# A two-block network with two expert layers on one core: row order and piece size of the expert weights, a two-part combine, a written order of TensorE's work, and a reordered first stage

## The chip, the core and the metric

The kernel runs on one core of one Trainium2 chip. The metric is device time of one execution in microseconds (us). Everything is fp32 data of one sequence: 512 tokens of width 1024, that is 581 MB of DMA traffic in all, most of it weights that are read once.

## What is computed

The network is two blocks in a row. Cut to what matters here:

```python
def first_block(x, ...):                       # one layer
    mod = silu(c) @ w_mod + b_mod              # sh1, s1, g1, sh2, s2, g2
    h = rms_norm(x, norm1_g) * (1 + s1) + sh1
    u = h @ w_pw1 + b_pw1; a, gate = split(u)  # conformer convolution
    u = dwconv(a * sigmoid(gate), w_dw) + b_dw # 31 taps, inside rows of 64 tokens
    y = silu(layer_norm(u)) @ w_pw2 + b_pw2
    x = x + g1 * y
    return x + g2 * (relu(modulated(x) @ w1) ** 2 @ w2)

def second_block(x, ...):                      # two layers
    x = x + g_m * mixer(l, modulated(x))       # l = 0: attention, l = 1: short convolution
    x = x + g_f * ec_moe(modulated(x), router_w, w_gate, w_up, w_down)

def ec_moe(h, w_router, w_gate, w_up, w_down): # 16 experts, each takes its 64 best tokens
    aff = softmax(h @ w_router)
    g, idx = top_k(aff.T, 64)
    xs = h[idx]
    a = silu(xs @ w_gate) * (xs @ w_up)        # 1024 x 1024 for each expert
    y = (a @ w_down) * g
    return zeros(n, d).at[idx].add(y)
```

The three weights of the 16 experts are 201 MB a layer, and all of them are read in every execution.

## The kernel before

**Frame.** The program is written in tiles; a planner places each engine's instructions in an order of its own, by estimated costs and by when the inputs are due. `keep_in_program_order(ins)` pins an instruction behind the one traced before it on the same engine; the kernel before doesn't use it for the experts. PSUM tiles come from two pools, `mm` (6 buffers) and `sm` (2). Large weights go through pages of 8 KB a partition (`wload` L207 to L216: 1 MiB a load, rows 128k to 128k+127, issued by SyncE).

**First stage** (`block1`, L502). Four loads bring x; TensorE transposes it (L515), DVE copies it (L516), ScalarE squares each transposed piece (L517), and eight matmuls with ones sum the squares over the features (L519). L522 to L528 make of that the row factor `rep`. The modulation `mod_now` (L256 matmuls, L263 turned to columns) gives s1 and sh1 by halves, `split` (L389, L390) the two parts of the modulated rows. A product of two fp32 matrices is done in three fp32r matmuls (L435 to L437), after a cast and a subtraction that split the weights (L428, L429). SyncE's loads go in program order: x, w_mod columns 2, 0, two pieces of w_pw1, w_mod 3, the rest of the constants, iota, and later w_mod 1, second pieces of w_pw1 with the bias rows b_pw1 and b_dw between them. b_pw1 is read with one row of 8 KB for each of 128 partitions.

**Convolution** (`conv`, `conv_half`). After the first products the weights of the depthwise convolution (31 x 1024) are loaded by ScalarE's queue into a page, and two matmuls with `taps` (L630) bring them to the frequency domain. `conv_half` (L683) multiplies each tile of 128 tokens (two rows of 64) with a DFT matrix for each row, with all 128 partitions contracted; the matrix holds zeros for the other row.

**Experts** (`moe`, L1292). The 16 experts go in 8 pairs (j, j+8): the two of a pair take the two column halves of TensorE, 64 tokens each. `gather` and `gather_part` select the tokens: a matmul spreads the list of indices (L1350), DVE compares it with iota (L1353, tile `o`), 32 matmuls (64 records) pick the rows (L1364) and DVE applies gain and shift (L1368). `gate_up` makes the gate product, silu (L1416), the up product and act = up * silu(gate) (L1420). `down` transposes act (L1432, ScalarE copies it, L1433), makes the down product, weighs its rows (L1439, L1440) and `combine`s them: 8 matmuls (16 records) add them to the tokens (L1447, L1449). Every product is 8 steps of 4 matmuls 128x64x512 (L1404), and each step waits for its own load from `eload` (L1394): 1 MiB, rows 128k to 128k+127 of both experts, 4 KB a row, one row of each expert to a partition. The pages, three blocks of halves, and two places in the pool of split weights hold these loads; a buffer comes free when its step is done, and SyncE issues the next load into it. The last pair of a layer (`down_last`, matmuls L1471) takes w_d by column halves, so that its first half can be combined while the second is loaded; these loads have pieces of 2 KB (L1391, 512 KB each). In layer 1 the product of the first half is followed by the final additions and the output.

## Time and profile before

| | |
|---|---|
| median of 3 runs | 2200.9 us (2199.98 to 2202.45) |
| the profiled execution | 2200.99 us, its span 2198.9 us |
| mean granted TensorE clock | 0.988 |
| expert stages | about 980 to 1470 us (layer 0), 1690 to 2199 us (layer 1) |
| DMA traffic | 581 MB |

The profile's page is of one execution, with times from the start of its span. A row of the timeline is one instruction or a run of like ones, with what ended the idle time before it in brackets. A window row gives the busy time of TensorE, its weight loads, VectorE, ScalarE and GpSimd (with their instruction counts), then the granted clock of TensorE (1.00 is 2.4 GHz, 0.50 is 1.2 GHz), the mean busy share of the 16 DMA engines, and what they moved in GB/s. An fp32 matmul shows as two records, an fp32r matmul as one. PE is TensorE, DVE VectorE, ACT ScalarE, POOL GpSimd, SP SyncE.

### The profile page before, as it was taken

The page shows a single profiled execution, that of the slowest core. Times are in us where ns is not written, and L with a number is a line of the kernel's source. Part 1 is how long each engine was busy: PE and PEld are TensorE (multiplying, and loading weights), DVE is VectorE, ACT ScalarE, POOL GpSimd, SP SyncE. Part 2 cuts the span into 40 slices and gives each one's busy share as a digit, 9 for nine tenths or more (in the row PEclk, how much of TensorE's full clock was granted, in tenths as well). Part 3 has the DMA queues.
Part 4 walks back from the last instruction along what each step waited for, and adds up shares of the span by engine and source line. Part 5 has one row for each costly group of instructions (what it writes and reads, how often), then busy time and mean ns, then how long its engine had stood idle before and what let it go on. Part 6 is the DMA issues. An engine that isn't in the chain of part 4 may idle for free.

```text
span 2198.9 us, 26994 instructions
## 1 busy us (share of the span) xinstructions
PE 2116.7 (96%) x11010; PEld 1353.5 (62%) x11010; DVE 1004.2 (46%) x1982; ACT 550.6 (25%) x1021; POOL 12.4 (1%) x12
## 2 busy tenths in 40 slices
PE   7999999999999989989999999989998999999998
PEld 4757878788888878765444444338886544444434
DVE  3868996778484579561122122135356122212211
ACT  2334534243343369520000000033232000000001
POOL 0000000000000000000000000010000000000000
PEclk9999999999999999999999999999998999999999
DMA  9715476677311352549999999992263999999996
GB/s 367 253 41 192 170 271 211 207 268 276 130 46 39 84 147 90 173 170 360 394 409 374 398 409 409 409 339 77 96 248 108 348 396 409 375 396 409 409 409 259
DMA packets 204379, 581.23 MB, mean 264 GB/s; under 512 B 12225, under 2 KB 21313, under 8 KB 204000
## 3 DMA queue, kind: packets, MB, share of 16 engines
q1 hardware_dynamic: 203936, 579.00, 70.5%
q8 instruction: 86, 1.41, 0.3%
q10 hardware_dynamic: 320, 0.52, 0.1%
q14 instruction: 37, 0.30, 0.0%
HBM read 571.48 MB, written 2.10 MB: 261 GB/s over the span
## 4 chain that ended last, share of the span: by engine, by line
PE 89%; DVE 4%; DMA 2%; ACT 1%; issue 0%; SPq 0%; DVEq 0%; ACTq 0%
PE mm L1404 29%; PE mm L436 13%; PE mm L435 13%; PE mm L437 13%; PE sm L1364 6%; PE mm L1447 5%; PE mm L1471 1%; PE sm L344 1%; PE tp L1126 1%; DMA b<-w_u 1%; PE sm L689 1%; PE sm L290 1%; DVE mx L1092 1%; PE sm L683 1%; PE sm L1432 1%; PE s L1089 1%
## 5 line engine op out<-in xcount | busy, mean ns | idle before, releaser
L435 PE MATMUL mm<-b,wh 128*128 128x512 f32 (+1 forms) x1136 | 391.6, 346 | 0.6 <-ACT ao L1131 0.5
L436 PE MATMUL mm<-b,wh 128*128 128x512 f32 (+1 forms) x1136 | 391.9, 345 | 0.0
L437 PE MATMUL mm<-b,wl 128*128 128x512 f32 (+1 forms) x1136 | 388.6, 343 | 0.5 <-DVE wl L429 0.5
L429 DVE TENSOR_TENSOR wl<-w,wh 128x1024 fp32r<-128x1024 f32 x160 | 194.1, 1223 | 173.1 <-ACT wh L428 171.9
L1404 PE MATMUL mm<-w,xs 128*64 128x512 f32 x1152 | 259.5, 599 | 0.0
L428 ACT CAST wh<-w 128x1024 fp32r<-128x1024 f32 x164 | 170.1, 1048 | 348.5 <-PE mm L436 266.1
L435 PEld LDWEIGHTS mm<-b,wh 128*128 128x128 f32 x1136 | 216.0, 190 | 39.1 <-issue 9.5
L436 PEld LDWEIGHTS mm<-b,wh 128*128 128x128 f32 x1136 | 216.4, 190 | 34.6 <-issue 9.5
L437 PEld LDWEIGHTS mm<-b,wl 128*128 128x128 f32 x1136 | 215.7, 190 | 28.1 <-issue 3.3
L1404 PE MATMUL mm<-b,xs 128*64 128x512 f32 x864 | 191.8, 593 | 0.0
L242 DVE SCALAR_TENSOR_TENSOR w<-w,sc 128x512 f32<-128x512 f32 x252 | 184.4, 750 | 3.5
L1404 PEld LDWEIGHTS mm<-w,xs 128*64 128x64 f32 x1152 | 82.2, 138 | 156.1 <-issue 148.5
L1420 DVE TENSOR_TENSOR ea<-mm,ea 128x512 f32<-128x512 f32 x32 | 22.1, 692 | 335.7 <-PE mm L1404 284.4
L1364 PEld LDWEIGHTS sm<-o,b 128*128 128x128 f32 x1024 | 121.5, 193 | 63.1 <-issue 55.3
L1364 PE MATMUL sm<-o,b 128*128 128x128 f32 x1024 | 135.6, 285 | 11.9 <-DVE o L1353 11.9
L1404 PEld LDWEIGHTS mm<-b,xs 128*64 128x64 f32 x864 | 67.4, 137 | 117.0 <-issue 102.5
L1368 DVE TENSOR_SCALAR xs<-sm,g_f,m_shf 128x128 f32<-128x128 f32 x128 | 45.9, 405 | 178.5 <-PE sm L1364 178.5
L435 PE MATMUL mm<-wh,b 128*128 128x512 f32 (+1 forms) x320 | 117.0, 370 | 2.9 <-ACT wh L428 2.9
L436 PE MATMUL mm<-wl,b 128*128 128x512 f32 (+1 forms) x320 | 117.8, 368 | 0.1
L437 PE MATMUL mm<-wh,b 128*128 128x512 f32 (+1 forms) x320 | 117.3, 366 | 0.0
L1404 PE MATMUL mm<-w,eaT 128*64 128x512 f32 x512 | 116.8, 598 | 0.0
L1447 PE MATMUL mm<-oT,ey 128*128 128x512 f32 (+1 forms) x248 | 108.1, 586 | 1.6 <-ACT ey L1477 1.6
(339 smaller groups left out, 2296.4 us busy)
## 6 DMA issues: line engine op xcount, KB each, us to landing
w<-w_g SPq DMA_DIRECT2D x80, 1024.0 KB, 17.3
w<-w_d SPq DMA_DIRECT2D x64, 1024.0 KB, 11.9
w<-w_u SPq DMA_DIRECT2D x64, 1024.0 KB, 14.2
b<-w_u SPq DMA_DIRECT2D x60, 1024.0 KB, 9.9
w<-ada_w SPq DMA_DIRECT2D x48, 1024.0 KB, 5.5
b<-w_g SPq DMA_DIRECT2D x48, 1024.0 KB, 16.0
b<-w_d SPq DMA_DIRECT2D x48, 1024.0 KB, 12.3
w<-w SPq DMA_DIRECT2D x32, 1024.0 KB, 6.3
```

Of the source, the lines that this page charges most:

```text
L242: nc.vector.scalar_tensor_tensor(acc, w[:, i], sc, acc, op0=ALU.mult, op1=ALU.add)
L290: nc.tensor.matmul(ps[32 * q:32 * q + 32], self.cst("ones")[:, :32], acc[:, q], start=True, stop=True, skip_group_check=True)
L428: self.nc.scalar.copy(vh, w[:, i:i + kp])
L429: (lo or self.nc.vector).tensor_tensor(vl, w[:, i:i + kp], vh.bitcast(F32), op=ALU.subtract)
L435: mm(out, sh, mh, start=start, stop=False)
L436: mm(out, sh, ml, start=False, stop=False)
L437: mm(out, sl, mh, start=False, stop=stop)
L1364: nc.tensor.matmul(ps[:, 128 * i:128 * i + 128], self.xn[:, t, 128 * k:128 * k + 128], o[:, t], start=(t == 0), stop=(t == 3), skip_group_ ...
L1368: nc.vector.tensor_scalar(xs[:, k], ps[:, 128 * i:128 * i + 128], self.fg[:, k:k + 1], self.fsh[:, k:k + 1], op0=ALU.mult, op1=ALU.add)
L1404: self.nc.tensor.matmul(ps[n][64 * b:64 * b + 64], lhs[:, k, 64 * b:64 * b + 64], w[b][:, 512 * n:512 * n + 512], start=(k == 0), stop=(k ...
L1420: nc.vector.tensor_tensor(act[:, c], up[n], act[:, c], op=ALU.mult)
L1447: nc.tensor.matmul(ps[:, :n], y[:, 128 * f:128 * f + 128], oT[:, t0:t0 + n], start=True, stop=True)
```

## The change

- **Experts, layout.** A partition now holds rows 8p to 8p+7 of a weight. A load brings two of these rows of one expert, 8 KB in one piece for a partition, 32 KB from one partition's piece to the next, and stays 1 MiB; a product waits for the loads of both experts at every second step. The other side of the contraction follows: act and the token-major rows xn are written in permuted columns (strided reads of PSUM in silu, in L1420 and in `token_major`), and gain and shift (`fgs`) are brought into that order through DRAM with three DMAs on GpSimd's queue when the routing begins. The last w_d is loaded in the same row order, pieces of 2 KB as before.
- **Combine.** The weighted rows are split in two fp32r parts (`weigh`: ScalarE writes the high part, VectorE what is left), and each tile takes two fp32r matmuls instead of one fp32 matmul.
- **TensorE's order.** From the end of a layer's first up product to the last pair's transposes, TensorE's expert matmuls are pinned as written: index matmul and first gather block (steps 0 to 3) after the up product, transposes (now in the `mm` pool), down product, second gather block (4 to 7), combine. The index list is padded to 128 partitions with a memset on GpSimd.
- **First stage.** ScalarE squares the token-major x with a running sum, so the sum matmuls L519 and L524 and their copy L522 are gone, and the row factor is made after the fourth transposed piece. The order of the loads changes: w_mod 2, the rest of the constants, w_dw (on ScalarE's queue, into another pool), w_mod 0, first pieces of w_pw1, w_mod 3; later both second pieces of w_pw1 before b_pw1, b_dw and iota. The tap matmuls move into the first stage.
- **DFT.** Each matmul of L683 contracts only the 64 partitions of its own row, in the `mm` pool.

The diff, cut to its core:

```diff
+    def pe(self, ins):
+        if self.pinned:
+            self.tc.keep_in_program_order(ins)
...
+        ms4 = self.sml.tile([128, 4], F32, name="ms4", bufs=1)
+        for t in range(4):
+            nc.scalar.activation(xn[:, 2 * t:2 * t + 2].rearrange("p f t -> p (f t)"), xt[:, t], AF.Square,
+                                 accum_out=ms4[:, t:t + 1])
+        nc.vector.tensor_scalar(ms4, ms4, 1.0 / D, None, op0=ALU.mult)
+        r = self.rsqrt(ms4, 4)
...
+            if f == 3:
+                rep = self.tmp.tile([128, T], F32, name="rep", tag="sl", bufs=2)
+                nc.vector.tensor_copy(rep, self.spread(r, 4))
...
-        ms, mh = [wm(2)], [wm(0)]
+        ms = [wm(2)]
+        nc.sync.dma_start(self.cs[:, NC0:], a["k_cst"][:, NC0:])
+        wd = self.wsp.tile([128, D], F32, name="wd", tag="wl")[:31]
+        nc.scalar.dma_start(wd, a["w_dw"])
+        mh = [wm(0)]
...
         ms.append(wm(3))
-        nc.sync.dma_start(self.cs[:, NC0:], a["k_cst"][:, NC0:])
...
+                rows = self.block(2)
+                for h in range(2):
+                    ps = self.sm_ps()
+                    nc.tensor.matmul(ps[:119], self.cst("taps", 31), wd[:, 512 * h:512 * h + 512], start=True, stop=True)
+                    nc.scalar.copy(rows[:119, 3 * D + 512 * h:3 * D + 512 * h + 512], ps[:119])
                 second = [self.wload(pw[0], 1, 4)]
+                row = lambda v, o, n: nc.sync.dma_start(rows[:, o:o + n], bass.AP(tensor=a[v].tensor, offset=0,
+                                                                                ap=[[0, 128], [1, n]]))
                 second.append(self.wload(pw[1], 1, 4))
+                row("b_pw1", 0, 2 * D)
+                row("b_dw", 2 * D, D)
+                nc.sync.dma_start(self.iota, a["k_iota"])
...
-        wd = self.page()[:31, :D]
-        nc.scalar.dma_start(wd, self.a["w_dw"])
-        for h in range(2):
-            ps = self.sm_ps()
-            nc.tensor.matmul(ps[:119], self.cst("taps", 31), wd[:, 512 * h:512 * h + 512], start=True, stop=True)
-            nc.scalar.copy(gf[:, 512 * h:512 * h + 512], ps[:119])
...
-                    p = self.sm_ps()
-                    o = fo + 119 * b
-                    nc.tensor.matmul(p[:119], self.cs[:, o:o + 119], u[:, t, c], start=True, stop=True)
+                    p = self.mm_ps()
+                    o, q = fo + 119 * b, slice(64 * b, 64 * b + 64)
+                    nc.tensor.matmul(p[:119], self.cs[q, o:o + 119], u[q, t, c], start=True, stop=True)
...
+        rows = self.dram.tile([2, D], F32, name="rows", tag="rows%d" % l)
+        self.fgs = self.sml.tile([128, 2, KT], F32, name="fgs", tag="fgs", bufs=1)
+        for i, v in enumerate((self.fg, self.fsh)):
+            nc.gpsimd.dma_start(rows[i].rearrange("(k p) -> p k", p=128), v)
+        nc.gpsimd.dma_start(self.fgs, rows.rearrange("i (p k) -> p i k", p=128))
...
+            self.best = self.sml.tile([128, 2, CAP], F32, name="best", tag="best", bufs=1)
+            nc.gpsimd.memset(self.best, 0.0)
+            nc.vector.tensor_copy(self.best[:NE], ps[:NE, 128:256].rearrange("p (i s) -> p i s", i=2))
...
+            self.pinned = True
             if j < 7:
                 gs = self.gather(j + 1)
-                for h in range(2):
-                    self.gather_part(gs, 4 * h, 4)
+                self.gather_part(gs, 0, 4)
...
-            self.down(l, j, act, end, after)
+            self.down(l, j, act, end, after, lambda: self.gather_part(gs, 4, 4))
...
-                nc.scalar.activation(self.xn[:, t, 512 * h:512 * h + 512], ps, AF.Copy, scale=r[:, i:i + 1])
+                nc.scalar.activation(self.xn[:, t].rearrange("p (k q) -> p k q", k=KT)[:, :, 64 * h:64 * h + 64],
+                                     ps.rearrange("p (q k) -> p k q", k=KT), AF.Copy, scale=r[:, i:i + 1])
...
-                nc.tensor.matmul(ps[:, 128 * i:128 * i + 128], self.xn[:, t, 128 * k:128 * k + 128], o[:, t],
-                                 start=(t == 0), stop=(t == 3), skip_group_check=True)
+                self.pe(nc.tensor.matmul(ps[:, 128 * i:128 * i + 128], self.xn[:, t, 128 * k:128 * k + 128], o[:, t],
+                                         start=(t == 0), stop=(t == 3), skip_group_check=True))
...
+    def eload(self, src):
+        t = self.eplace()
+        if isinstance(t, list):
+            for k in range(2):
+                self.nc.sync.dma_start(t[k], src[:, k])
+            return t
+        v = t.rearrange("p (k n) -> p k n", k=2)
+        self.nc.sync.dma_start(v, src)
+        return [v[:, k] for k in range(2)]
+
+    def rows(self, name, l, e):
+        return self.a[name][l, e].rearrange("(p k) n -> p k n", k=KT)
...
-            w = self.eload(self.a[name][l, j::8, 128 * k:128 * k + 128, :])
+            if k % 2 == 0:
+                w = [self.eload(self.rows(name, l, j + 8 * b)[:, k:k + 2]) for b in range(2)]
             for n in range(2):
                 for b in range(2):
-                    self.nc.tensor.matmul(ps[n][64 * b:64 * b + 64], lhs[:, k, 64 * b:64 * b + 64],
-                                          w[b][:, 512 * n:512 * n + 512],
-                                          start=(k == 0), stop=(k == KT - 1), skip_group_check=True)
+                    self.pe(self.nc.tensor.matmul(ps[n][64 * b:64 * b + 64], lhs[:, k, 64 * b:64 * b + 64],
+                                                  w[b][k % 2][:, 512 * n:512 * n + 512],
+                                                  start=(k == 0), stop=(k == KT - 1), skip_group_check=True))
...
+        av = act.rearrange("p (k q) -> p k q", k=KT)
         for n in range(2):
-            nc.scalar.activation(act[:, 512 * n:512 * n + 512], gp[n], AF.Silu)
+            nc.scalar.activation(av[:, :, 64 * n:64 * n + 64], gp[n].rearrange("p (q k) -> p k q", k=KT), AF.Silu)
...
-            nc.vector.tensor_tensor(act[:, c], up[n], act[:, c], op=ALU.mult)
+            c = slice(64 * n, 64 * n + 64)
+            nc.vector.tensor_tensor(av[:, :, c], up[n].rearrange("p (q k) -> p k q", k=KT), av[:, :, c], op=ALU.mult)
...
-            ps = self.sm_ps()
+            ps = self.mm_ps()
...
-                nc.tensor.transpose(ps[:, 128 * i:128 * i + 128], act[:, 128 * k:128 * k + 128], self.cst("ident"))
+                self.pe(nc.tensor.transpose(ps[:, 128 * i:128 * i + 128], act[:, 128 * k:128 * k + 128], self.cst("ident")))
...
-        y = self.wsp.tile([128, D], F32, name="ey", tag="wh")
+        y = tuple(self.wsp.tile([128, D], F32R, name="y" + i, tag="w" + i) for i in "hl")
...
         if j == 7:
+            self.pinned = False
         dp = self.product("w_d", l, j, aT)
-        nc.scalar.activation(y[:, :512], dp[0], AF.Copy, scale=w)
-        nc.vector.tensor_scalar(y[:, 512:], dp[1], w, None, op0=ALU.mult)
+        mid()
+        for n in range(2):
+            self.weigh(y, dp[n], w, slice(512 * n, 512 * n + 512))
         self.combine(y, oT, 0, T, range(KT))
+
+    def weigh(self, y, ps, w, c):
+        yh, yl = y
+        self.nc.scalar.activation(yh[:, c], ps, AF.Copy, scale=w)
+        self.nc.vector.scalar_tensor_tensor(yl[:, c], ps, w, yh[:, c].bitcast(F32), op0=ALU.mult, op1=ALU.subtract)
...
-            nc.tensor.matmul(ps[:, :n], y[:, 128 * f:128 * f + 128], oT[:, t0:t0 + n], start=True, stop=True)
+            for i in range(2):
+                self.pe(nc.tensor.matmul(ps[:, :n], y[i][:, 128 * f:128 * f + 128], oT[:, t0:t0 + n],
+                                         start=(i == 0), stop=(i == 1)))
...
+            for i in range(4):
+                v = self.eplace().rearrange("p (e k n) -> p e k n", e=2, k=2)
+                for e in range(2):
+                    nc.sync.dma_start(v[:, e], self.rows("w_d", l, j + 8 * e)[:, 2 * i:2 * i + 2, 512 * n:512 * n + 512])
+                ws.append([v[:, e] for e in range(2)])
```

## Rows read from the trace of the kernel before

**Rows 1.** Page, busy time of each engine over the span (share) and instruction counts.

```profile
PE 2116.7 (96%) x11010; PEld 1353.5 (62%) x11010; DVE 1004.2 (46%) x1982; ACT 550.6 (25%) x1021; POOL 12.4 (1%) x12
```

**Rows 2.** Waits of SyncE over the whole run: engine, line, releaser: total us, times, longest us.

```profile
SPq L1394 <- PE mm L1404: 653.3, 243, 23.4
```

**Rows 3.** Timeline of ScalarE, layer 0 experts: start us, us, instruction, idle before and releaser.

```profile
1001.19 0.60 ACT L1416 ACTIVATE ea<-mm 128x512 f32<-128x512 f32 x1 [29.32 <-PE mm L1404]
...
1060.10 0.60 ACT L1416 ACTIVATE ea<-mm 128x512 f32<-128x512 f32 x1 [20.26 <-PE mm L1404]
...
1312.04 0.60 ACT L1416 ACTIVATE ea<-mm 128x512 f32<-128x512 f32 x1 [20.26 <-PE mm L1404]
...
1372.99 0.60 ACT L1416 ACTIVATE ea<-mm 128x512 f32<-128x512 f32 x1 [20.26 <-PE mm L1404]
...
1423.07 0.60 ACT L1416 ACTIVATE ea<-mm 128x512 f32<-128x512 f32 x1 [20.26 <-PE mm L1404]
```

**Rows 4.** Windows of 10 us, layer 0 experts: busy us per engine, PEclk, DMA share, GB/s.

```profile
1050.00:1060.00 10.00, 10.00 (x50) 3.40 (x48) 0.00 (x0) 0.00 (x0) 0.00 (x0) 1.00 0.89 322
1170.00:1180.00 10.00, 10.00 (x34) 3.85 (x34) 6.86 (x11) 0.00 (x0) 0.00 (x0) 1.00 0.69 247
1240.00:1250.00 10.00, 10.00 (x48) 3.30 (x46) 0.00 (x0) 0.00 (x0) 0.00 (x0) 1.00 0.95 343
1300.00:1310.00 10.00, 10.00 (x48) 3.30 (x46) 0.79 (x3) 0.00 (x0) 0.00 (x0) 1.00 1.03 410
1440.00:1450.00 10.00, 8.89 (x33) 2.73 (x30) 0.00 (x0) 2.75 (x4) 0.00 (x0) 1.00 1.05 386
```

**Rows 5.** Chain of waits at the end of layer 0: start us, us, what.

```profile
1416.94 18.44 DMA b<-w_u
1435.39 10.79 DMA w<-w_d
```

**Rows 6.** Timeline of one pair whose gather stands in one piece, layer 0.

```profile
1076.11 7.41 PE L1364 MATMUL sm<-o,b 128*128 128x128 f32 x64 [0.88 <-DVE o L1353]
...
1084.63 0.65 PE L1432 MATMUL sm<-cs,ea 128*128 128x128 f32 x4 [0.68 <-ACT eaT L1433]
```

**Rows 7.** Chain of waits, layer 0, one combine.

```profile
1169.45 7.06 PE mm L1447 x16
```

**Rows 8.** Chain of waits, convolution stage: matmuls of the split products.

```profile
126.14 0.43 PE mm L437
...
130.97 0.23 PE mm L437
```

**Rows 9.** Windows of 1 to 5 us: start, convolution, end of layer 1.

```profile
24.00:28.00 4.00, 3.65 (x24) 1.37 (x22) 2.50 (x8) 0.24 (x1) 0.00 (x0) 1.00 1.05 386
41.00:42.00 1.00, 1.00 (x8) 0.73 (x5) 0.00 (x0) 0.00 (x0) 0.00 (x0) 1.00 1.05 428
42.00:43.00 1.00, 1.00 (x6) 0.83 (x5) 0.00 (x0) 0.00 (x0) 0.00 (x0) 1.00 1.02 422
120.00:121.00 1.00, 0.00 (x0) 0.00 (x0) 1.00 (x3) 0.00 (x0) 0.00 (x0) 1.00 0.06 25
125.00:130.00 5.00, 5.00 (x12) 3.70 (x12) 0.00 (x0) 0.58 (x1) 0.00 (x0) 0.50 0.79 276
2174.00:2176.00 2.00, 2.00 (x9) 0.60 (x7) 0.27 (x1) 0.00 (x0) 0.00 (x0) 1.00 0.46 171
```

**Rows 10.** Chain of waits, layer 1, first half of the last w_d product.

```profile
2165.01 7.04 PE mm L1471 x32
```

**Rows 11.** Groups by line: matmuls of the DFT and of the taps.

```profile
L683 PE MATMUL sm<-b,cs 128*119 128x512 f32 x32 | 16.1, 610 | 0.0
...
L630 PE MATMUL sm<-w,cs 31*119 31x512 f32 x4 | 2.7, 814 | 3.9 <-DMA w<-w_dw 3.9
```

**Rows 12.** Timeline of the first stage: row factor, first split product.

```profile
26.29 0.69 DVE L528 COPY rep<-sm 128x512 f32<-128x512 f32 x1 [1.25 <-PE sm L378]
...
32.41 2.07 PE L435 MATMUL mm<-wh,b 128*128 128x512 f32 x4 [2.56 <-ACT wh L428]
```

## What was predicted, and how

> **What bounds the kernel now.** I read the page's busy times first: TensorE is busy for 96% of the span, no other engine for half of it [rows 1]. That is an average, so I went to the stages that the change touches most, the two expert stages, and asked who waits for whom. SyncE, which issues the weight loads, waits 243 times for an expert matmul to free a buffer [rows 2]: TensorE is behind, the loads ahead. The first silu of a pair marks its gate product: seven steps from 1001.19 to 1423.07 are 421.9 us, 60.3 each; a pair with its gather in one piece takes 58.9, one whose gather the planner mixed into a product 60.95, the pair without a gather 50.1 [rows 3]. Layer 1 repeats these steps. The windows then show how thin the lead is: three have the DMA below its rate (322, 247, 343), the others stand at 409 to 410 GB/s with a share above 1.0 [rows 4]. A pair needs 24 loads of 1 MiB, 25.17 MB; over 60.3 us that is 417 GB/s, more than the 409 that arrive. So the stage starts on full buffers, is paced by TensorE, and uses up its lead: the chain at the end of layer 0 has 18.4 and 10.8 us of DMA [rows 5]. **Whatever shortens TensorE's pair makes the loads the bound; their rate decides the size of the gain.**
>
> **Experts, TensorE's side.** A gather is 64 records in 7.4 us [rows 6], the combine 16 records in 7.06 us [rows 7]. The two-part combine still has 16 records (two for each of 8 tiles), but of the kind that the split products issue, 0.23 us at the full clock [rows 8]: 3.7 us, 3.4 less a pair. The pin gives back the 2 us by which a mixed pair is longer than one in block order. The transposes in the larger pool lose the 0.7 us wait for the copy of the first four [rows 6]. A pair is then 58.9 - 3.4 - 0.7, about 55 us of TensorE, or 25.17 MB / 55 = 458 GB/s of demand. Two waits are added. The low part of the weighted rows (DVE) waits for the high part (ACT), and behind it on DVE stand the combine's adds, which free TensorE's tiles: some 1.5 us, covered by the gather's second block (half of 7.4), uncovered it would be 1.5 a pair. And the product waits for two loads every second step, so buffers come free later: up to 1 MiB of lead, 2.6 us, once. Strided PSUM reads go to ACT and DVE, which have room [rows 1]. The round trip of the gain rows on GpSimd's queue is issued when the routing begins, long ahead of the first gather, and only a memset stands behind it: nothing; uncovered, a few us a layer.
>
> **Experts, the loads.** The same bytes in the same number of issues, in pieces of 8 KB in place of 4. The nearest rows: pieces of 2 KB run at 386 GB/s, of 4 KB at 409, and the one load with 8 KB pieces (a row that is broadcast) at 428 and 422 [rows 4, 9]. Over 16 engines a piece takes 16 x 2048 / 386 = 85 ns and 16 x 4096 / 409 = 160 ns; another 4 KB on the same slope, 150 ns, makes 310 ns, or 422 GB/s. I take 421, with ends 409 (no gain) and 428. **So the stage becomes DMA-bound:** 421 supplied against 458 wanted. What that gives:
> Idle time of the queue is gone: (409 - 322) / 409 x 10 = 2.1, then 4.0 and 1.6 us from the three windows [rows 4], 7.7 in sum. (A dip in the first pair stays, since the buffers are still full there.)
> Otherwise the queue runs from the first pair, about 1030, to 1435.4 [rows 5]: 397 us x (1 - 409 / 421) = 11.3 us.
> The last w_d keeps its 2 KB pieces. The last combine saves some 3 us in two halves and gives about 1 back to the second weighing step, which nothing covers there: 2.
> Layer 0: -21 us.
> Layer 1: the loads end 7.7 + 11.3 = 19 us earlier. Here TensorE runs behind them to the end: w_d is in by about 2175 [rows 9], so its first half (4.19 MB, 10.8 us at 387) by 2164.2, but the product of that half runs from 2165.0 to 2172.05 without a pause [rows 10]. After the change the half is in by 2145.2 and its product ends one load's matmuls later, 0.9 us, 2146.1; the tail behind it stays: -26 us. TensorE's own limit, 7 x (60.3 - 55) = 37 us less, is not reached in either layer.
>
> **Weights of the depthwise convolution.** TensorE waits 3.9 us for them, and the tap matmuls then take 2.7 [rows 11]. After that pause its granted clock is 0.50, the lower of its two levels [rows 9], and eleven records take 0.43 instead of 0.23 [rows 8], 2.2 us, with half a microsecond more for the one before them. Loaded at the start, all of that goes: -9. The price there: the load moves 25 GB/s at a share of 0.06, one engine of sixteen [rows 9], for about 5 us, in a stretch where all sixteen are full (1.05 [rows 9]); what SyncE queues behind it on that engine can land up to 5 us later. The tap matmuls stand where TensorE waits 2.6 us for ACT [rows 12]; uncovered they cost 1.4 to 2.7 us.
>
> **Row halves in the DFT.** 32 records, 16.1 us [rows 11]. If two 64-row halves run side by side, half of their time, 7 to 8 us, can go; if not, nothing. No row shows such a pair, but the experts' two column halves do run together: 32 records in 7.04 us [rows 10], where the combine needs 7.06 for 16 [rows 7]. DVE, which reads each tile, is next; I take -3.
>
> **First stage.** The sum matmuls and their copy are gone, and the row factor can be there some 3 us before 26.3 [rows 12]. But the large part of the constants now goes in front of w_mod(0) (0.37 MB, 1 us), as does w_dw (up to 5 us); the second loads of w_pw1 pass the bias rows and iota, which are wanted later. Between -3 and +6 I take -1.
>
> **Sum**, against the profiled execution's own 2200.99 us (2.1 us of it outside the span; the median of the runs is 2200.9, so nothing is corrected): 21 + 26 + 9 + 3 + 1 = 60, so 2141 us.
>
> **Rivals.**
> A, larger pieces bring nothing: 409 as before. For it: the queue's share is above 1.0 already. Against: the broadcast row. Then layer 0 keeps 7.7 + 2 = 9.7; in layer 1 the half of w_d is in by 2156.5, its product done by 2157.4, 14.7 less. With 13 from the front: 2201 - 37.4 = 2164.
> The Trainium skill ("DMA: Bandwidth & Descriptors", "Where 436 GB/s comes from") says that between HBM and SBUF the memory side, about 358 GB/s, is what binds. By that no size of piece could help, and the time would be A's; but this trace moves 409 and 428 GB/s [rows 4, 9], above that limit, and the measurement decides.
> B, the loads run at 428: the second term is 397 x (1 - 409 / 428) = 17.6, 6.3 more a layer: 2128, and TensorE's limit lets it go little further.
> C, slower than before. A partition's pieces now lie 32 KB apart, where the old load read 4 KB rows one behind the other. If that pitch costs the queue, each layer pays. At 387 the second term is 397 x (409 / 387 - 1) = +22.6: layer 0 +12.9, layer 1 +7.9, less 13, 2209. The sign turns at about 391 GB/s; at 370 (+42 a layer) it is 2247, and I price C there. Against it: w_mod, whose rows lie 24 KB apart, loads at the same 386 as the last w_d with rows 4 KB apart [rows 4, 9].
> The same page ("Latency and other measured facts") gives 207 GB/s for copies with a row pitch of 512 KiB and less at larger powers of two. No run here shows such a pitch, and 32 KB is not among its cases.
> D, the front gives nothing: the load on one engine holds up the first products, the halves do not pair: 2201 - 47 = 2154.
>
> **Chances.** The forecast (2130 to 2150) 0.60, A 0.15, B 0.10, D 0.08, C 0.07. The range goes to A and B with the unknowns of the front (3 down, 6 and more up) around them: 2118 to 2175. About 0.2%, 4.4 us, is what a measurement can tell here from no change; all cases but C are faster by more, and near C's turning point lies the little that is left: faster 0.91, same 0.02, slower 0.07.
>
> **What would show it.** Right: windows of the expert stages at about 421 GB/s with no dips after the first pair; SyncE's waits for expert matmuls mostly gone, and TensorE's for w_g, w_u, w_d in their place; marks some 59.8 us apart (25.17 / 421); the combine 16 records in 3.7 us; no wait for w_dw and no clock of 0.50 near 125. Wrong: windows at 409 (A), marks nearer 55 (B), windows under 391 (C), the first split product later than 32.4 (D). Wrong altogether: a clock that falls in many short waits for loads, which the DMA-bound end of layer 0 does not show (1.00 at 8.9 us busy of 10 [rows 4]), or a pinned matmul that waits for DVE's adds where the planner had other work.

## The result, and the profile after

The changed kernel takes 2148.9 us (median of 4 runs, 2146.0 to 2150.8) against 2201.7 us for the kernel before: a ratio of 0.976, 95% interval 0.9744 to 0.9775. The forecast was 2141, so the sign and most of the size came out as worked out, with 8 us too much gain. The profiled execution has a span of 2148.2 us. (Line numbers below are those of each kernel's own program. In the changed kernel L1426 is the expert products, L1411 their loads, L1440 the silu, L1509 the last w_d, L1381 the gather.)

Busy time, from the page, to be held against [rows 1]: TensorE lost 74 us, the span 51.

```profile
PE 2043.2 (95%) x10986; PEld 1353.0 (63%) x10986; DVE 1004.7 (47%) x1998; ACT 558.5 (26%) x1035; POOL 18.0 (1%) x20
```

SyncE's waits for the expert matmuls, against the 243 of [rows 2]; 97 are left:

```profile
SPq L1411 <- PE mm L1426: 308.3, 97, 27.7
```

The first silu of some pairs of layer 0 (timeline of ScalarE), against [rows 3]. The four steps to 1212.40 take 55.1 to 55.5 us each, the fifth 56.7, the last two 60.9 and 59.7:

```profile
990.98 0.60 ACT L1440 ACTIVATE ea<-mm 128x512 f32<-128x512 f32 x1 [29.51 <-PE mm L1426]
...
1046.11 0.60 ACT L1440 ACTIVATE ea<-mm 128x512 f32<-128x512 f32 x1 [19.75 <-PE mm L1426]
...
1212.40 0.60 ACT L1440 ACTIVATE ea<-mm 128x512 f32<-128x512 f32 x1 [19.78 <-PE mm L1426]
...
1269.10 0.60 ACT L1440 ACTIVATE ea<-mm 128x512 f32<-128x512 f32 x1 [19.75 <-PE mm L1426]
...
1329.95 0.60 ACT L1440 ACTIVATE ea<-mm 128x512 f32<-128x512 f32 x1 [19.74 <-PE mm L1426]
...
1389.61 0.60 ACT L1440 ACTIVATE ea<-mm 128x512 f32<-128x512 f32 x1 [19.77 <-PE mm L1426]
```

Windows of 10 us in layer 0 (columns as in [rows 4]): two dips in the first pairs, then a level queue.

```profile
1010.00:1020.00 10.00, 9.76 (x53) 4.09 (x54) 1.37 (x4) 1.07 (x2) 0.00 (x0) 1.00 0.86 343
1030.00:1040.00 10.00, 10.00 (x48) 4.61 (x48) 6.43 (x12) 0.00 (x0) 0.00 (x0) 1.00 0.91 359
1100.00:1110.00 10.00, 10.00 (x50) 3.42 (x48) 0.00 (x0) 1.19 (x2) 0.00 (x0) 1.00 1.01 420
1300.00:1310.00 10.00, 10.00 (x51) 3.48 (x46) 0.64 (x1) 1.16 (x2) 0.00 (x0) 1.00 1.02 420
```

So the stage has two parts. While the first buffers last, TensorE sets the pace at the 55 us worked out for its pair; when the lead is gone, after five pairs, the loads set it at 59.7 to 60.9 us, where 25.17 MB / 421 is 59.8. The rate is the 420 to 421 GB/s that the slope of [rows 9] gave.

Time by stage, read at the same instruction in both traces:

| from, to | before | after | change | forecast |
|---|---|---|---|---|
| start to the first split product | 32.4 | 36.1 | +3.7 | -1 |
| to the first DFT matmul | 100.7 | 90.5 | -10.2 | -9 |
| to the first silu of layer 0 | 868.1 | 864.4 | -3.7 | -3 |
| to the first silu of layer 1 | 719.3 | 702.6 | -16.7 | -21 |
| to the end of the span | 478.4 | 454.6 | -23.8 | -26 |

The first row is no firmer than some 3 us: in the four traces that keep the old first stage (before and three of the experiments) the first split product comes at 32.4, 34.3, 35.1 and 35.5 us, so the trace of before is the earliest of them.

### The profile page after: what moved, and what is told of

The parts are those of the page before. It is cut to its first block, busy times and chain, and to the rows that moved or that the text cites. A ratio compares the mean times of both kernels' runs of the same rounds, so it can differ in the third digit from the quotient of the medians.

```text
span 2148.2 us, 26989 instructions
## 1 busy us (share of the span) xinstructions
PE 2043.2 (95%) x10986; PEld 1353.0 (63%) x10986; DVE 1004.7 (47%) x1998; ACT 558.5 (26%) x1035; POOL 18.0 (1%) x20
## 5 line engine op out<-in xcount | busy, mean ns | idle before, releaser
L1426 PE MATMUL mm<-w,xs 128*64 128x512 f32 x1152 | 263.8, 600 | 13.2 <-DMA w<-w_u 13.2
L1426 PE MATMUL mm<-b,xs 128*64 128x512 f32 x864 | 198.4, 594 | 3.7 <-DMA b<-w_u 3.5
L1426 PEld LDWEIGHTS mm<-w,xs 128*64 128x64 f32 x1152 | 84.7, 138 | 175.1 <-issue 140.3
L1426 PEld LDWEIGHTS mm<-b,xs 128*64 128x64 f32 x864 | 69.0, 137 | 123.8 <-issue 102.2
L1381 PEld LDWEIGHTS sm<-o,b 128*128 128x128 f32 x1024 | 118.8, 194 | 34.8 <-DVE o L1370 16.0
L1381 PE MATMUL sm<-o,b 128*128 128x128 f32 x1024 | 126.3, 282 | 13.8 <-DVE o L1370 13.8
L1473 DVE SCALAR_TENSOR_TENSOR yl<-mm,scol,yh 128x512 fp32r<-128x512 f32 x30 | 22.5, 751 | 213.2 <-ACT yh L1472 211.5
L1426 PE MATMUL mm<-w,eaT 128*64 128x512 f32 x512 | 112.7, 594 | 1.9 <-ACT eaT L1457 1.9
L1440 ACT ACTIVATE ea<-mm 128x512 f32<-128x512 f32 x32 | 19.1, 597 | 343.2 <-PE mm L1426 343.2
```

What stands on the lines that cost most here:

```text
L1381: self.pe(nc.tensor.matmul(ps[:, 128 * i:128 * i + 128], self.xn[:, t, 128 * k:128 * k + 128], o[:, t], start=(t == 0), stop=(t == 3), ski ...
L1426: self.pe(self.nc.tensor.matmul(ps[n][64 * b:64 * b + 64], lhs[:, k, 64 * b:64 * b + 64], w[b][k % 2][:, 512 * n:512 * n + 512], start=(k ...
L1473: self.nc.vector.scalar_tensor_tensor(yl[:, c], ps, w, yh[:, c].bitcast(F32), op0=ALU.mult, op1=ALU.subtract)
```

## The experiments

Each is a change to one of the two kernels. All times are medians; the ratio behind a time, with its 95% interval, is to runs of the kernel before on the same chip (2201.5 to 2202.5 us). "The changed kernel" is the one with the whole change, at 2148.9 us.

**Size of the pieces.** The changed kernel with the old row order: the rearrangement of `rows`, and the layouts of act, xn, gain and shift with it.

```diff
-        return self.a[name][l, e].rearrange("(p k) n -> p k n", k=KT)
+        return self.a[name][l, e].rearrange("(k p) n -> p k n", p=128)
```

> The changed kernel with one part taken back: the expert weights lie in the old row order again (a load brings two rows 128 apart of one expert, pieces of 4 KB), with act, xn, gain and shift in the old column order; pin, two-part combine, waits for two loads and the front stay. Theory 1 (after the change the loads set the pace of both expert stages, at 421 GB/s): windows fall to 409 GB/s, each layer takes 397 us x (421/409 - 1), about 11 us more, so 2149 + 22 = 2171 us (2167 to 2175), marks of the late pairs 61.5 us apart. Theory 2 (the gain is TensorE's shorter pair, pieces do not matter): 2149 us, within 3.

Measured: 2165.6 us, 0.9837 (0.9817 to 0.9856), 16.7 more than the changed kernel, and just under the range of theory 1. A window of layer 0, and two late marks 62.2 us apart:

```profile
1300.00:1310.00 10.00, 9.76 (x61) 5.24 (x62) 1.36 (x4) 1.07 (x2) 0.00 (x0) 1.00 1.03 410
```

```profile
1275.84 0.60 ACT L1433 ACTIVATE ea<-mm 128x512 f32<-128x512 f32 x1 [19.76 <-PE mm L1419]
...
1338.01 0.60 ACT L1433 ACTIVATE ea<-mm 128x512 f32<-128x512 f32 x1 [19.78 <-PE mm L1419]
```

The seven steps of layer 0 grow by 9.3 us and those of layer 1 by 9.2, near the 11 of the expectation. Layer 0 gives 5 us back behind its last silu, because in this run its end is not made longer by ScalarE (below). Theory 2 falls: with TensorE's order and combine untouched, the pieces, with the layouts that go with them, are worth 17 us.

**The pin.** The changed kernel without it.

```diff
-            self.pinned = True
```

> The changed kernel without the pin: the planner orders TensorE's work in a pair again. Theory 1 (loads set the pace): a pair is some 57 us of TensorE, still under 59.8, so within 3 us of 2149; if the end of layer 1 again gets its transposes (turn back of the tokens) into the up product's waits, 2 to 4 us less. Theory 2 (the order is a main part of the gain): pairs 2 us longer through the whole layer, 7 x 2 x 2 = 28, about 2177 us.

Measured: 2214.8 us, 1.0061 (1.0044 to 1.0078). That is 66 us more than with the pin, over twice what even theory 2 allowed, and slower than before. The later pairs take 63.5 us:

```profile
1191.66 0.60 ACT L1439 ACTIVATE ea<-mm 128x512 f32<-128x512 f32 x1 [30.27 <-PE mm L1425]
...
1255.14 0.60 ACT L1439 ACTIVATE ea<-mm 128x512 f32<-128x512 f32 x1 [30.27 <-PE mm L1425]
```

The timeline of TensorE and its weight loads (PEld) in such a pair shows where the time goes. Six matmuls, 12 records, take 3.65 us, where 16 records take as long in the changed kernel; most of the weight loads come one by one, 0.43 us apart, and not two at a time:

```profile
1235.30 3.65 PE L1425 MATMUL mm<-b,xs 128*64 128x512 f32 x12
...
1237.07 0.14 PEld L1425 LDWEIGHTS mm<-b,xs 128*64 128x64 f32 x1 [0.29 <-issue]
1237.49 0.14 PEld L1425 LDWEIGHTS mm<-b,xs 128*64 128x64 f32 x1 [0.29 <-issue]
1237.92 0.14 PEld L1425 LDWEIGHTS mm<-b,xs 128*64 128x64 f32 x1 [0.29 <-issue]
```

This is the planner's order for TensorE at one such place, read from the program that this kernel builds. The weights w_13381 belong to the first expert and w_13383 to the second, two steps to a load:

```
L1425 MATMUL mm_13357<-w_13381   first expert, left half of the result
L1425 MATMUL mm_13358<-w_13381   first expert, right half
L1380 MATMUL sm_13715<-o_13712   x6, gather
L1425 MATMUL mm_13357<-w_13383   second expert, left
L1425 MATMUL mm_13358<-w_13383   second expert, right
L1425 MATMUL mm_13357<-w_13381   from here on the two experts alternate
L1425 MATMUL mm_13357<-w_13383
```

The load of the second expert is due later, and the planner draws the first expert's matmuls ahead. Two matmuls on the same column half then follow each other and run one after the other. The four main groups of expert products (2912 records) are busy for 727.5 us in this run, against 659.6 in the changed kernel: 68 us, about as much as the difference of the two times. The largest group of each, this run first:

```profile
L1425 PE MATMUL mm<-w,xs 128*64 128x512 f32 x1152 | 294.5, 602 | 0.0
...
L1426 PE MATMUL mm<-w,xs 128*64 128x512 f32 x1152 | 263.8, 600 | 13.2 <-DMA w<-w_u 13.2
```

**The rows alone.** The kernel before with the new row order, loads by expert and the layouts that go with them, without pin, two-part combine and new front.

```diff
-            w = self.eload(self.a[name][l, j::8, 128 * k:128 * k + 128, :])
+            if k % 2 == 0:
+                w = [self.eload(self.rows(name, l, j + 8 * b)[:, k:k + 2]) for b in range(2)]
```

> The kernel before with one part of the change: row order, 8 KB pieces and loads by expert; no pin, fp32 combine, old front. Theory 4 (with loads by expert the planner puts both column halves of a tile's first expert ahead of the second expert's, the two no longer run side by side, and only the pin keeps them together): pairs of some 66 us, 7 x 2 x 6 = 84 us slower than before, 2270 to 2300. Theory 1 as the prediction had it (TensorE's pair stays at 60.3, the loads get faster): layer ends earlier by what the chain showed of DMA, 2185 to 2200 us.

Measured: 2276.1 us, 1.0335 (1.0318 to 1.0352), as theory 4 has it. Two marks are 67.7 us apart, where the kernel before has 60.95 [rows 3]; the four groups of expert products are busy for 732.7 us against 657.9, 75 us more, where the whole kernel takes 74 more:

```profile
1272.29 0.60 ACT L1430 ACTIVATE ea<-mm 128x512 f32<-128x512 f32 x1 [20.31 <-PE mm L1417]
...
1339.99 0.60 ACT L1430 ACTIVATE ea<-mm 128x512 f32<-128x512 f32 x1 [20.31 <-PE mm L1417]
```

**No pin, loads for both experts.** The test of that mechanism: no pin either, but a load brings one row of both experts.

```diff
-            self.pinned = True
...
-            if k % 2 == 0:
-                w = [self.eload(self.rows(name, l, j + 8 * b)[:, k:k + 2]) for b in range(2)]
+            v = self.eplace()
+            src = self.a[name][l, j::8].rearrange("e (p k) n -> p e k n", k=KT)[:, :, k]
...
+                v = v.rearrange("p (e n) -> p e n", e=2)
+                self.nc.sync.dma_start(v, src)
+                w = [[v[:, e]] * 2 for e in range(2)]
```

> The changed kernel without the pin, with loads that bring one row of both experts (rows 8p+k, 4 KB pieces, 1 MiB, one step each); everything else as changed. Theory 4 (the planner parts the two experts only because their loads are separate): products stay paired, pairs of about 57 us of TensorE, then the loads at 409 GB/s: 2165 to 2185 us, some 35 less than without the pin and with loads by expert (2215). Rival (the planner's mixing of gather and product is itself what costs): pairs above 63 us, 2205 to 2220.

Measured: 2171.9 us, 0.9867 (0.9852 to 0.9882); marks 58.3 us apart:

```profile
1233.55 0.60 ACT L1447 ACTIVATE ea<-mm 128x512 f32<-128x512 f32 x1 [25.17 <-PE mm L1433]
...
1291.84 0.60 ACT L1447 ACTIVATE ea<-mm 128x512 f32<-128x512 f32 x1 [25.17 <-PE mm L1433]
```

The run gives back 43 of the 66 us, though its pieces are 4 KB again, which alone cost 17 in the first experiment. The four groups of expert products are back at 665.4 us. So mixing gather and product is not what costs 66 us; parting the two experts is. With the loads by expert that 8 KB pieces bring, the pin is a condition of the gain. With loads for both experts it was not tried, but there is little left for it: the pinned run with 4 KB pieces, the first experiment, is 6 us faster than this one.

**The combine.** The changed kernel with one fp32 matmul a tile, and the rows weighed as before.

```diff
...
-            for i in range(2):
-                self.pe(nc.tensor.matmul(ps[:, :n], y[i][:, 128 * f:128 * f + 128], oT[:, t0:t0 + n],
-                                         start=(i == 0), stop=(i == 1)))
+            self.pe(nc.tensor.matmul(ps[:, :n], y[:, 128 * f:128 * f + 128], oT[:, t0:t0 + n], start=True, stop=True))
...
```

> The changed kernel with the combine in one fp32 matmul a tile as before; all else as changed. Theory 1 (loads set the pace): the pair is 55.4 + 3.4 = 58.8 us of TensorE, just under the loads' 59.8; only the first four pairs and the last combine of layer 0 get longer, the queue has some more idle time while buffers are full: 2151 to 2159 us. Theory 2 (TensorE sets the pace): 2 x 7 x 3.4 = 48 us more, about 2196 us.

Measured: 2168.2 us, 0.9849 (0.9833 to 0.9865): 19.3 more than the changed kernel, between the two theories. The pair is 58.7 us, as worked out, to the last mark of layer 0:

```profile
1341.78 0.60 ACT L1440 ACTIVATE ea<-mm 128x512 f32<-128x512 f32 x1 [23.83 <-PE mm L1426]
...
1400.48 0.60 ACT L1440 ACTIVATE ea<-mm 128x512 f32<-128x512 f32 x1 [23.83 <-PE mm L1426]
```

Theory 1 had left out the lead. At 58.7 a pair takes only 1.1 us from it, so TensorE sets the pace to the end of the layer (410.4 us for seven steps in place of 398.6) and the loaded buffers are never used up. A bound of 59.8 us holds only for what the lead does not cover.

**The load of w_dw in the first stage.** The changed kernel with that load behind those of w_pw1's second value columns, and the tap matmuls back where the kernel before has them.

```diff
-        wd = self.wsp.tile([128, D], F32, name="wd", tag="wl")[:31]
-        nc.scalar.dma_start(wd, a["w_dw"])
...
-        wa = list(self.pieces(self.wload(self.a["w_pw1"][:, 512:D])))
+        wa = self.wload(self.a["w_pw1"][:, 512:D])
+        wd = rows[:31, 3 * D:]
+        nc.sync.dma_start(wd, self.a["w_dw"])
+        wa = list(self.pieces(wa))
...
```

> The changed kernel with the load of w_dw taken out of the first stage: SyncE issues it behind the loads of the second half of w_pw1's value columns (about 60 us, when the queue runs empty), straight into the rows that the tap matmuls overwrite, and the tap matmuls stand where they stood before the change. Theory 3 (the load on one engine, issued first of all, is what delays x, the constants and w_mod, by some 4 us): identity there at 6.4 instead of 12.1 us, first split product at 30 to 32.4 instead of 36.1, no wait for w_dw at 118, 2143 to 2146 us. Rival (the new order of the constants, or the squares on ScalarE, delay the start): first split product stays near 36, 2149 to 2151 us.

Measured: 2144.9 us, 0.9741 (0.9725 to 0.9757), 4.0 less than the changed kernel. The start of the changed kernel, where ScalarE issues the load first of all and the constants are there at 12.1 us:

```profile
0.74 0.53 ACTq L541 DMA_DIRECT2D wd<-w_dw  x1
...
12.10 4.24 PE L528 MATMUL mm<-cs,b 128*128 128x128 f32 x24 [12.10 <-DMA cs<-k_cst]
...
36.13 2.08 PE L442 MATMUL mm<-wh,b 128*128 128x512 f32 x4 [2.55 <-ACT wh L435]
```

and of this one:

```profile
6.39 4.99 PE L528 MATMUL mm<-cs,b 128*128 128x128 f32 x24 [6.39 <-DMA cs<-k_cst]
...
30.51 2.07 PE L442 MATMUL mm<-wh,b 128*128 128x512 f32 x4 [2.56 <-ACT wh L435]
```

The constants come 5.7 us earlier, and the first split product 5.6. Since single traces of one first stage differ by some 3 us here, all of them together say what it is worth: the first split product comes at 32.4 to 35.5 us in the four traces with the old first stage (mean 34.3), at 34.8 to 37.6 in the five with that of the change (35.9), at 28.1 to 30.5 in the three with w_dw late (29.3). So the new first stage gives some 5 us by itself, and the load on one engine of sixteen takes that away and 1.6 us more, as rival D had it for the first products.

**w_dw alone.** The kernel before with that load moved to the same place.

```diff
+        wd = rows[:31, 3 * D:]
+        nc.sync.dma_start(wd, self.a["w_dw"])
...
-        wd = self.page()[:31, :D]
-        nc.scalar.dma_start(wd, self.a["w_dw"])
```

> The kernel before with w_dw alone moved: SyncE issues it behind the loads of the second value columns of w_pw1, near 60 us; the first stage is untouched. Theory (the wait of 3.9 us and the half clock behind it are the price of that load): no wait near 118, clock 1.00 from 120 to 130, 2192 us (2190 to 2195). Rival (TensorE only waits elsewhere, for the tiles of DVE): 2197 or more.

Measured: 2196.5 us, 0.9968 (0.9958 to 0.9978), 6 less than before and between the two theories. The wait and the low clock of [rows 9] are gone:

```profile
120.00:125.00 5.00, 5.00 (x24) 4.14 (x23) 4.89 (x9) 0.00 (x0) 0.00 (x0) 1.00 0.00 0
125.00:130.00 5.00, 5.00 (x21) 3.43 (x19) 4.80 (x8) 1.26 (x2) 0.00 (x0) 1.00 0.74 216
```

From the first split product to the first DFT matmul it is 93.2 us in place of 100.7, 7.4 less, where the wait and the half clock had cost 6.6. The first DFT matmul is only 4.8 us earlier, because in this trace the first split product itself comes 2.7 us later (35.1 against 32.4), which is within the spread of that stage. So the load cost 7.4 us at its place.

**Row halves alone.**

```diff
-                    p = self.sm_ps()
-                    o = fo + 119 * b
-                    nc.tensor.matmul(p[:119], self.cs[:, o:o + 119], u[:, t, c], start=True, stop=True)
+                    p = self.mm_ps()
+                    o, q = fo + 119 * b, slice(64 * b, 64 * b + 64)
+                    nc.tensor.matmul(p[:119], self.cs[q, o:o + 119], u[q, t, c], start=True, stop=True)
```

> The kernel before with the DFT matmuls alone split by row halves, in the larger PSUM pool. Theory (two row halves run side by side): four records in 1.1 us instead of 1.9, 8 x 0.8 = 6 us of TensorE, of which waits for DVE take up to 4 back: 2195 to 2199 us. Rival (nothing pairs): 2201.

Measured: 2201.1 us, 0.9996 (0.9986 to 1.0005): no difference. Four records take 1.12 us instead of 1.88, so the halves do run together (before, then this run):

```profile
133.08 1.88 PE L683 MATMUL sm<-b,cs 128*119 128x512 f32 x4
...
135.86 1.12 PE L683 MATMUL mm<-b,cs 64*119 64x512 f32 x4
```

The group takes 12.0 us in place of 16.1, but TensorE now waits for DVE's tiles behind it:

```profile
PE sm L689 <- DVE w L686: 3.4, 2, 2.6
```

In the changed kernel the same group is 11.9 us with 3.8 us of wait in front of it, 15.7 together:

```profile
L690 PE MATMUL mm<-b,cs 64*119 64x512 f32 x32 | 11.9, 696 | 3.8 <-DVE b L616 3.8
```

**The ends of the expert stages.** Three edits on top of the late w_dw: own loads for the last two steps of the last up product, the table load of layer 0 behind the copies of act, and three turned-back tiles (the tokens, transposed back for the output) of layer 1 in the last up product, with the transposes of act there in the pool `sm` (the first two edits are shown with the next run).

```diff
+        if l == 1 and j == 7:
+            back = lambda k: self.xp0.extend(self.turn_back(0, [k // 2])) if k in (0, 2, 4) else None
-        up = self.product("w_u", l, j, xs)
+        up = self.product("w_u", l, j, xs, back, j == 7)
```

> The changed kernel with w_dw late as in the run before, and the ends of the expert stages mended: the last two steps of the last up product get their own loads of both experts (4 KB pieces, as each step of the kernel before), the table load of ScalarE at the end of layer 0 comes behind the copies of the transposed act, and three of the four turned-back tiles of layer 1 stand in the last up product. Theory 5 (what fell short of the forecast is work of TensorE and ScalarE between the last w_u and the first half of w_d): layer 0 gains 1.8 + 2.8 + 1.9 (no half clock), layer 1 some 5: 2145 - 10 = 2135 us (2131 to 2139). Rival (the loads of w_d end both stages anyway): 2142 to 2146.

Measured: 2143.3 us, 0.9736 (0.972 to 0.9752), as the rival had it and not to be told from the run with w_dw late alone. By the marks, though, layer 0 took 6.2 us less (696.6 in place of 702.8), and layer 1 lost 3.8: 458.4 us from its first silu to the end, against 454.6. There TensorE now works without a pause through the last up product: the tiles had moved, not vanished.

The same without the turned-back tiles and their pool:

```diff
-            elif l == 0:
-                with self.logs_table():
-                    self.nc.scalar.copy(self.sml.tile([128, 1], F32, name="done", bufs=1), act[:, 1023:])
...
+            if fine and k >= 6:
+                v = self.eplace().rearrange("p (e n) -> p e n", e=2)
+                for e in range(2):
+                    self.nc.sync.dma_start(v[:, e], self.rows(name, l, j + 8 * e)[:, k])
+                w = [[v[:, e]] * 2 for e in range(2)]
...
+            if l == 0:
+                with self.logs_table():
+                    self.nc.scalar.copy(self.sml.tile([128, 1], F32, name="done", bufs=1), aT[:, 7, 127:])
```

> The changed kernel with w_dw late, own loads for the last two steps of the last up product in both layers, and the table load behind the copies of act in layer 0; the turned-back tiles of layer 1 stay where the change has them. Theory 5a (layer 0 ends with what ScalarE and the two-step loads put between the last w_u and w_d; layer 1 ends with TensorE's own work, so that moving its tiles ahead only moved the queue): layer 0 as in the run before (about 6 us less than with w_dw late alone), layer 1 some 1 to 2 less and no longer tail: 2145 - 7 = 2138 us (2135 to 2141). Rival (layer 0's gain is given back in layer 1, as in the run before): 2143.

Measured: 2140.0 us, 0.9721 (0.9708 to 0.9734): faster than both kernels, and in the range of theory 5a. Against the run with w_dw late alone, layer 0 takes 696.8 us, 6.0 less, as expected; layer 1 takes 456.3 us, 1.7 more, where theory 5a had 1 to 2 less and the rival nearly 4 more. The last w_d product of layer 0 waits 0.24 us for the copies and runs at the full clock:

```profile
1403.31 6.43 PE L1514 MATMUL mm<-w,eaT 128*64 128x512 f32 x26 [0.24 <-ACT eaT L1459]
...
1405.04 1.28 ACT L377 ACT_TABLE_LOAD   x1 [1.30 <-DMA w<-w_d]
```

## Why the prediction was right, and where it was not

**What bounds the stage: right for the loads, too simple for the pace.** The changed stage ends DMA-bound at the forecast 421 GB/s. Three piece sizes now lie on one line: 85, 160 and 16 x 8192 / 421 = 311 ns. Rival A falls by the 17 us of the first experiment, rival C by the rate: pieces 32 KB apart cost the queue nothing here. The Trainium skill ("DMA: Bandwidth & Descriptors", "Where 436 GB/s comes from") puts what binds loads from HBM at about 358 GB/s. These runs move 421, so here the measurement decides against it. But the sign "marks some 59.8 us apart" holds only for the last two of seven steps. The first four lie near 55 us, which the prediction had listed as a sign of rival B, though the rate is 421: there the lead still covers the loads. And TensorE's pair counts as much as the rate does: 3.3 us more of it cost 19 us in the combine's experiment, where a stage bound by its loads alone was expected to lose 2 to 10.

**The pair of TensorE: right in size, wrong in one reason.** The pair is 55.4 us (55 forecast), the combine 3.3 less. But the step on the pin, "gives back the 2 us by which a mixed pair is longer", failed: it was worked out from pairs whose loads bring both experts. There it is near: without a pin and with such loads the pair takes 58.3 us, 2.9 more than the pinned one. With loads by expert the pin holds 66 us, because the planner would part the halves that run together. The trace of before could not show it, but the diff did: the product's weights became two tiles with two due times. The forecast held only because the change carries the pin: as far as its reason goes, that is luck.

**Idle time of the queue.** Two dips stayed in the first pair, (421 - 343) / 421 x 10 = 1.9 and 1.5 us, since TensorE still sets the pace there. The forecast had taken the dip of the first pair as unchanged; by the same working it was 4.6 us before (windows of 236 and 392 GB/s at 1020 and 1030), so nothing is lost by it. The reading that all other windows of before stand at 409 to 410 passed over one: 377 at 1180, another 0.8 us.

**The end of layer 0: failed (-16.7, not -21).** The loads came as forecast: the queue turns to the 2 KB pieces of the last w_d some 20 us earlier, counted from the first silu (windows of 2 us, at 1433 before and 1403 after). The step on the last combine, a gain of 2 us, left out what stands between the last w_u and w_d. Timeline of the changed kernel:

```profile
1399.92 3.65 PE L1426 MATMUL mm<-b,xs 128*64 128x512 f32 x16 [1.31 <-DMA b<-w_u]
...
1404.92 3.65 PE L1426 MATMUL mm<-b,xs 128*64 128x512 f32 x14 [1.35 <-DMA b<-w_u]
...
1409.43 1.09 PE L1456 MATMUL mm<-cs,ea 128*128 128x128 f32 x8 [0.85 <-DVE ea L1444]
1410.93 1.28 ACT L377 ACT_TABLE_LOAD   x1 [19.85 <-PE mm L1456]
...
1412.66 1.07 ACT L1457 COPY eaT<-mm 128x512 f32<-128x512 f32 x2 [0.24 <-ACTq L376]
...
1413.30 8.78 PE L1509 MATMUL mm<-w,eaT 128*64 128x512 f32 x32 [2.78 <-ACT eaT L1457]
```

The last two steps wait for one pair of loads, and 3.65 us of product follow it, where before it was one step; ScalarE's table load (1.28 us) and a small copy stand ahead of both copies of act, 2.78 us of wait; and behind this wait the granted clock falls:

```profile
1414.00:1416.00 2.00, 2.00 (x8) 0.57 (x6) 0.00 (x0) 0.00 (x0) 0.00 (x0) 0.57 1.05 388
1416.00:1418.00 2.00, 2.00 (x8) 0.55 (x6) 0.00 (x0) 0.00 (x0) 0.00 (x0) 0.57 1.05 385
1418.00:1420.00 2.00, 2.00 (x12) 0.72 (x10) 0.00 (x0) 0.00 (x0) 0.00 (x0) 1.00 1.05 386
```

0.57 is near the lower of the two levels, and 32 records take 8.78 us, not the 7.04 of [rows 10]. It goes with the wait for ScalarE: in the combine's experiment the only long wait is the one for ScalarE, 2.18 us, and the window of 5 us from 1420 has a clock of 0.67; in the first experiment it waits three times 1.5 us for loads and not for ScalarE, and the clock stays at 1.00. The prediction had named a clock "that falls in many short waits for loads" as what would make it wrong altogether, and held it off with the end of layer 0 before [rows 4], where no wait is so long; the one wait that mattered was not for a load. The last experiment takes the two-step loads and the table load out of the way; the clock then stays at 1.00, and 6.0 us come back.

**The end of layer 1: partly (-23.8, not -26).** The step "its product ends one load's matmuls later" failed. That step looked at the load and at nothing behind it. The chain of the changed kernel has, behind the last load of w_u:

```profile
2087.71 19.91 DMA b<-w_u
...
2107.66 3.66 PE mm L1426 x14
...
2112.17 1.09 PE mm L1456 x8
2113.26 3.57 PE mm L1551 x32
2116.83 8.73 PE mm L1509 x40
```

3.7 us of a two-step product, the transposes, 3.6 us of turned-back tiles, then the whole first half of w_d without a wait: TensorE's work, not the load, ends it. Moving the tiles ahead only moved TensorE's queue. The tail behind it is 2.7 us shorter in the changed kernel (15.5 us between the two weighing steps, 18.1 in the kernel before and in the last two experiments). There the planner has put 12 records of turned-back tiles behind the last product, where the others have 4 and TensorE waits 0.85 us for ScalarE. This order was not varied by itself, and the prediction had the tail unchanged: without this gain layer 1 would be at -21.

**The front (-10.2, not -13).** Between the first split product and the first DFT matmul, where the load of w_dw was, it is -10.2 of -9, and this is firm: 100.4 to 100.7 us in the three traces with the old load, 89.2 to 90.6 in the five with the changed one. It is the 7.4 us of w_dw alone and the 2.7 of the tap matmuls, which now stand in the first stage. But it is +3.7 at the start (some +1.6 by the means of all traces), where the prediction had written "up to 5 us" and taken -1. That choice was the mis-sized term; the late load gets 4 us of it back. The Trainium skill ("DMA: Bandwidth & Descriptors", "Why a DMA increments its semaphore by 16 and not by 1") says that a load uses the largest number of engines, up to 16, that divides the slowest dimension of both its sides: for 31 rows, one engine. The share of 0.06 in [rows 9] agrees.

The term of the row halves, -3, came out as -3.7 in its stage, but that is a number without its mechanism. On the same stretch the halves alone give 0.9 us (867.2 against 868.1), and the DFT group with its waits takes 15.7 us against 16.1. What shortens the rest of that stretch was not followed; this fit is luck.

## To carry to other kernels

Before an edit that splits one load into two, ask what the planner or the program order kept together because the operands arrived together: here 66 us hung on matmuls of two experts staying side by side. A stage that starts on full buffers becomes DMA-bound only when its lead is used up, so work out both paces and the lead, and not the larger pace alone. And a small load that fits one engine belongs where the queue is empty, not ahead of loads that need all sixteen.

## What was not expected of the hardware

Pieces of 8 KB at a pitch of 32 KB run at 417 to 426 GB/s in windows of 10 us, with a share of 1.01 to 1.02, on the line of the smaller ones. Two matmuls on 64-row halves run together: four records in 1.12 us against 1.88. Two matmuls on the two column halves do so only while they stay side by side in the order: parted, the expert products took 68 us more. A load of 124 KB on one engine, issued first, moved the arrival of the first constants from 6.4 to 12.1 us. And at the end of layer 0, where TensorE had waited 2.8 us for ScalarE, the granted clock was 0.57 for about the next 4 us (1414 to 1418).
